# A two-layer diffusion backbone on one core: the first stage with TensorE's order written out, tokens loaded where the low parts go, seven strip buffers, and selector products for the strips' sums

## The chip, the cores and the metric

One core of a Trainium2 chip runs the whole program. The metric is the device time of one execution in microseconds, median of the runs; the profile shows one more execution of the same program. TensorE is called PE below, VectorE DVE, ScalarE ACT, GpSimd POOL, and SP is the engine that issues most of the loads.

## The reference

512 tokens (256 latent, 256 context) of width 2048 go through two layers. Layer 0 is bidirectional retention, layer 1 windowed attention. Each layer begins alike: an RMS norm of the tokens, times a gain and a scale, plus a shift, where scale, shift and a later gate are products of SiLU(c) with a large matrix `ada_w`, one set for the latent tokens and one for the context.

```python
c_act, cc_act = jax.nn.silu(c), jax.nn.silu(c_ctx)
...
mod_l = c_act @ ada_w[i] + ada_b[i]          # mod_c likewise from cc_act
sh_l, sc_l, gt_l = jnp.split(mod_l, 3, axis=-1)
h_l = _rms_norm(x, norm_gain[i]) * (1 + sc_l[:, None]) + sh_l[:, None]
h_c = _rms_norm(ctx, norm_gain[i]) * (1 + sc_c) + sh_c
...
p = h @ w_in                                  # queries, keys, values, gate of layer 0
```

## The kernel before, in words

Everything is held transposed: width on the partitions in 16 blocks of 128 (called kb), the 512 tokens along the free axis. A float32 product is made of three products of a rounded type: each operand is split into a high part and a low part (`split`, L109 to L111: ACT casts to the high part at L110, DVE subtracts at L107), and `mm3` (L126 to L132) issues high times high, high times low and low times high. Weights come in pieces of 128 x 1024 (512 KB) through `load_w` (L120): three raw buffers, three high and three low ones.

The **first stage**, which the change rewrites, is L273 to L390. It does four things.

- *Tokens.* Eight DMAs bring the tokens into `xT`. ACT squares each of 16 blocks (L323, L326), DVE adds the squares up (L327), and `token_rstd` (L220) turns the sum into one factor per token: four products with a column of ones (L228), a power on POOL (L217), four transposes (L233). ACT copies the result to `rB` (L329). Between the adds DVE works through a chain of small operations for the decays of the retention (L290 to L317), which POOL's powers interrupt.
- *Strips.* `strip_part(u, g)` brings a quarter of the ada_w columns of two blocks (1 MB, `araw`, four buffers, L344) and multiplies it with the padded SiLU(c) (L346): four products side by side, each into 32 rows of one PSUM tile. After the fourth quarter ACT copies the tile (L351), PE transposes it in four pieces (L355), DVE sums the four groups of rows (L358), adds the bias and makes shift and gain (`ada_mod`, L248).
- *Modulation.* For each block and each kind of token (L236 to L245): DVE scales (L241), ACT adds the shift and rounds to the high part (L243), DVE makes the low part (L244).
- *Products.* The queries' and keys' columns of head 0 and of the next chunk: two weight pieces per pair of blocks. The first piece accumulates in four PSUM tiles through all 16 blocks (`qk0`); the second starts anew for each pair of blocks, and DVE adds each finished tile to `qk1` in SBUF (L386). Five PSUM tiles have the tag acc; `qk0` holds four of them through the stage, so that the second piece's tiles go through the one that is left, and the last of four through a tile of the tag pm (three in all, shared with the strips and transposes).

The loop runs over 64 groups (8 pairs of blocks x 2 pieces x 4 column slices), and a table (`DUE`) says before which group a quarter of the next strip is issued. The framework's scheduler then decides how the instructions of each engine stand; each engine carries its own out in order. SP's loads stand in one queue too: a load that has no free buffer holds all behind it. After the stage, the values' chunk starts (`gemm_ts`, L180), and the rest of the program follows.

Of the kernel before, what the change touches and what calls it, by code (L numbers as in the profile page):

```python
# [20 lines left out]
KB = 16  # L21
# [5 lines left out]
DUE = (0, 2, 4, 5)  # L27
DUE0 = (0, 2, 4, 5)
# [20 lines left out]
V_END = V_KG + 128  # L49
# [3 lines left out]
def backbone(ctx: ExitStack, tc, xT_d, w0_d, wo0_d, w1_d, wo1_d, adaS_d, adaB_d,  # L53
# [46 lines left out]
    hT = r1.tile([P, 2, KB, T], F32R, name="hT")  # L100
    hT_h, hT_l = hT[:, 0], hT[:, 1]


    h1 = hT.rearrange("p a k t -> p (a k t)").rearrange("p (k s a t) -> p k s a t", k=KB, s=2, a=2)
# [22 lines left out]
    def mm3(ps, a, b, start, stop, skip=False):  # L127

        (ah, al), (bh, bl) = a, b
        nc.tensor.matmul(ps, lhsT=ah, rhs=bh, start=start, stop=False, skip_group_check=skip)  # L130
        nc.tensor.matmul(ps, lhsT=ah, rhs=bl, start=False, stop=False, skip_group_check=skip)  # L131
        nc.tensor.matmul(ps, lhsT=al, rhs=bh, start=False, stop=stop, skip_group_check=skip)  # L132
# [26 lines left out]
    def gemm_ws2(w_d, chunk, nkp, s, hook=None, pre=None):  # L159
# [3 lines left out]
        for kp in range(nkp):  # L163
# [3 lines left out]
            for j in range(4):  # L167
                js = slice(j * P, (j + 1) * P)
                for k2 in range(2):
                    kb = 2 * kp + k2  # L170
                    nc.tensor.matmul(accs[j], lhsT=wh[:, k2, js], rhs=h1[:, kb, s].rearrange("p a t -> p (a t)"),  # L171
                                     start=(kb == 0), stop=False)
                    nc.tensor.matmul(accs[j][:, 0:L], lhsT=wl[:, k2, js], rhs=h1[:, kb, s, 0],  # L173
# [21 lines left out]
    def h_mov(kb):  # L195
        return hT_h[:, kb, :], hT_l[:, kb, :]

    def h_stat(kb, t):
        s = slice(t * P, (t + 1) * P)
        return hT_h[:, kb, s], hT_l[:, kb, s]  # L200

    def h1_stat(kb, t):
        s = slice(t % 2 * P, (t % 2 + 1) * P)
        return h1[:, kb, t // 2, 0, s], h1[:, kb, t // 2, 1, s]
# [15 lines left out]
    def token_rstd(pool, parts, blocks=(0, 4)):  # L220
# [10 lines left out]
        bp = m_tile()  # L231
        for t in range(n):
# [3 lines left out]
    def modulate(t, src, kb, gs, sh, rB, kinds=(0, 1), layer=0):  # L236

        for s in kinds:
            c = slice(s * L, (s + 1) * L)
            hi, lo = (h1[:, kb, s, 0], h1[:, kb, s, 1]) if layer else (hT_h[:, kb, c], hT_l[:, kb, c])  # L240
            nc.vector.scalar_tensor_tensor(out=t[:, c], in0=src[:, c], scalar=gs[:, kb, s:s + 1],  # L241
                                           in1=rB[:, c], op0=ALU.mult, op1=ALU.mult)
            nc.scalar.activation(hi, t[:, c], AF.Identity, bias=sh[:, kb, s:s + 1])  # L243
            nc.vector.scalar_tensor_tensor(out=lo, in0=t[:, c], scalar=sh[:, kb, s:s + 1],  # L244
                                           in1=hi.bitcast(F32), op0=ALU.add, op1=ALU.subtract)  # L245

# [26 lines left out]

    with tc.tile_pool(name="pa", bufs=1) as pa:
        xT = pa.tile([P, KB, T], F32, name="xT")
        for i in range(8):
            nc.sync.dma_start(out=xT[:, 2 * i:2 * i + 2, :], in_=xT_d[:, 2 * i:2 * i + 2, :])
        nc.sync.dma_start(out=cst, in_=cst_d)


        nc.scalar.activation(cact.rearrange("p k t -> p (k t)"), vec[:, V_C:V_C + 32], AF.Silu)
        cpad = wide("aacc1", "cpad").rearrange("p (k t) -> p k t", t=32)
        nc.gpsimd.memset(cpad, 0.0)
        nc.vector.tensor_copy(cpad[:, :, 0:2], cact)

# [33 lines left out]

        ssq = wide("rows", "ssq")  # L320
        for i in range(KB):
            if i == 0:
                nc.scalar.activation(ssq, xT[:, 0, :], AF.Square)  # L323
                continue
            sq = wide("pt", "sq", 2)
            nc.scalar.activation(sq, xT[:, i, :], AF.Square)  # L326
            nc.vector.tensor_tensor(out=ssq, in0=ssq, in1=sq, op=ALU.add)  # L327
        rB = wide("aacc0", "rB")
        nc.scalar.copy(rB, token_rstd(pb, [ssq]))  # L329


        units = [[2 * k, 2 * k + 1] for k in range(8)]
        strips = {}

        def strip_part(u, g):
# [4 lines left out]
            if g == 0:  # L340
                strips[u] = m_tile()
            ap_ = strips[u]
            raw = pa.tile([P, 4, 512], F32, name="araw", tag="araw", bufs=4)
# [4 lines left out]
            if g < 3:  # L348
                return
# [644 lines left out]
```

## Time and profile before

| | us |
|---|---|
| median of 3 runs (2017.89 to 2020.73) | 2019.93 |
| the profiled execution, by the same clock | 2020.57 |
| its span, first to last instruction | 2018.6 |
| first product of the stage with tokens, L130 | starts at 34.48 |
| first product of the values' chunk | starts at 161.76 |

Rows of the time line have the start in us, the duration, the engine, the line, the operation, what it writes and reads, a count, and in brackets how long the engine had sat idle before and what ended that. A row with a count above one merges neighbours, and its duration is the time that they cover. Products are pipelined, so that the distance from one start to the next, not the duration, is what one costs. Rows of the table by stretches have, behind the stretch, the busy time and the count for PE, its weight loads, DVE, ACT and POOL, and then the clock granted to PE, the share of the DMA engines, and GB/s.

### The profile page before, as it was taken

To read this page: it belongs to the slowest core of one execution; us is meant where nothing else is said; L and a number is where in the kernel's file an instruction comes from. 1 tells how busy PE (TensorE), PEld (TensorE's weight loads), DVE (VectorE), ACT (ScalarE), POOL (GpSimd) and SP (SyncE) were. 2 spreads that over 40 slices of the span, in tenths; PEclk is the share of its full clock that TensorE was granted. 3 is DMA by queue.
4 is the path that set the end of the run, shared out by engine and by line. 5 is a ranking of instruction groups with operands and counts; after the bars stand their busy time and mean duration, and the time that the engine had idled before them with its cause. 6 is when DMAs were issued, how large, how long until landed. Compare 5 with 4: busy or idle time off the path is not lost.

```text
span 2018.6 us, 24747 instructions
## 1 busy us (share of the span) xinstructions
PE 1986.9 (98%) x9312; PEld 1620.5 (80%) x9312; DVE 1160.1 (57%) x2324; ACT 708.4 (35%) x1080; POOL 239.7 (12%) x89
## 2 busy tenths in 40 slices
PE   5999999999999999999999999999999999999999
PEld 2558888888888888888888888888888888888887
DVE  4556323778678688686465244432232665777754
ACT  3224223233232232232332233422221434766653
POOL 6500402203104004004000000000000010000001
PEclk9999999999999999999999999999999999999999
DMA  9873224565556656555555334733333334444455
GB/s 362 334 267 111 86 92 150 180 197 168 183 176 189 183 170 188 183 179 181 188 183 163 113 104 147 265 121 99 110 105 95 104 98 147 139 141 130 151 190 168
DMA packets 112711, 330.10 MB, mean 164 GB/s; under 512 B 12112, under 2 KB 18384, under 8 KB 107856
## 3 DMA queue, kind: packets, MB, share of 16 engines
q1 hardware_dynamic: 103376, 315.94, 48.0%
q10 hardware_dynamic: 9216, 12.59, 1.7%
q8 instruction: 73, 1.20, 0.2%
q14 instruction: 46, 0.38, 0.1%
HBM read 315.90 MB, written 12.58 MB: 163 GB/s over the span
## 4 chain that ended last, share of the span: by engine, by line
PE 96%; DVE 1%; DMA 1%; issue 0%; ACT 0%; POOL 0%; SPq 0%; DVEq 0%; POOLq 0%; ACTq 0%
PE acc L130 26%; PE acc L131 25%; PE acc L132 25%; PE acc L171 6%; PE acc L173 3%; PE pm L130 2%; PE pm L131 2%; PE pm L132 2%; PE pm L346 2%; DMA wraw<-uT_d 1%; PE pm L843 1%; PE pm L560 1%; DVE ssq L327 0%; DMA xT<-in_xT 0%; PE pm L773 0%
## 5 line engine op out<-in xcount | busy, mean ns | idle before, releaser
L107 DVE TENSOR_TENSOR wl<-wraw,wh 128x1024 fp32r<-128x1024 f32 x368 | 451.2, 1227 | 621.6 <-ACT wh L110 621.0
L110 ACT CAST wh<-wraw 128x1024 fp32r<-128x1024 f32 x368 | 386.9, 1052 | 948.4 <-PE acc L132 494.1
L130 PE MATMUL acc<-wh,hT 128*128 128x512 f32 x1280 | 501.5, 392 | 0.0
L132 PE MATMUL acc<-wh,hT 128*128 128x512 f32 x1280 | 498.7, 390 | 0.0
L131 PE MATMUL acc<-wl,hT 128*128 128x512 f32 x1280 | 498.6, 390 | 0.0
L439 DVE SCALAR_TENSOR_TENSOR ajunk<-abraw,crow 128x512 bf16<-128x512 f32 x448 | 308.8, 689 | 11.2 <-ACT crow L428 2.8
L130 PE MATMUL acc<-hT,wh 128*128 128x512 f32 x752 | 298.1, 397 | 2.6 <-ACT wh L110 1.9
L131 PE MATMUL acc<-hT,wh 128*128 128x512 f32 x752 | 294.8, 392 | 0.0
L132 PE MATMUL acc<-hT,wl 128*128 128x512 f32 x752 | 289.8, 390 | 0.0
L132 PEld LDWEIGHTS acc<-wh,hT 128*128 128x128 f32 x1280 | 240.2, 188 | 50.9 <-DVE hT L244 0.7
L130 PEld LDWEIGHTS acc<-wh,hT 128*128 128x128 f32 x1280 | 240.5, 188 | 48.4 <-issue 0.3
L131 PEld LDWEIGHTS acc<-wl,hT 128*128 128x128 f32 x1280 | 240.5, 188 | 48.4 <-DVE wl L107 0.2
L502 POOL TENSOR_TENSOR dd<-two,dd 128x128 f32<-128x128 f32 x8 | 167.5, 20944 | 601.6 <-DVE dd L500 601.6
L130 PEld LDWEIGHTS acc<-hT,wh 128*128 128x128 f32 x752 | 141.6, 188 | 53.7 <-DVE qk L386 7.2
L171 PE MATMUL acc<-hT,wh 128*128 128x512 f32 x512 | 182.7, 399 | 0.0
L131 PEld LDWEIGHTS acc<-hT,wh 128*128 128x128 f32 x752 | 141.7, 188 | 32.1 <-issue 4.2
L132 PEld LDWEIGHTS acc<-hT,wl 128*128 128x128 f32 x752 | 141.3, 188 | 30.3 <-issue 0.8
L217 POOL TENSOR_TENSOR rs<-ms,mhalf 128x1 f32<-128x1 f32 (+2 forms) x47 | 40.8, 868 | 1023.6 <-DVE ms L211 673.7
L173 PE MATMUL acc<-hT,wl 128*128 128x256 f32 x512 | 144.0, 281 | 0.0
L171 PEld LDWEIGHTS acc<-hT,wh 128*128 128x128 f32 x512 | 96.2, 188 | 22.7
L173 PEld LDWEIGHTS acc<-hT,wl 128*128 128x128 f32 x512 | 96.7, 189 | 0.7
L131 PE MATMUL acc<-r_l,wh 128*128 128x512 f32 (+1 forms) x188 | 70.7, 376 | 0.0
(208 smaller groups left out, 1836.4 us busy)
## 6 DMA issues: line engine op xcount, KB each, us to landing
wraw<-in_w SPq DMA_DIRECT2D x272, 512.0 KB, 3.5
abraw<-in_adaB SPq DMA_DIRECT2D x256, 256.0 KB, 3.3
wraw<-in_wo SPq DMA_DIRECT2D x96, 512.0 KB, 3.5
araw<-in_adaS SPq DMA_DIRECT2D x32, 1024.0 KB, 7.5
uT_d<-ue ACTq DMA_DIRECT2D x32, 256.0 KB, 2.1
wraw<-uT_d SPq DMA_DIRECT2D x16, 512.0 KB, 4.1
xT<-in_xT SPq DMA_DIRECT2D x8, 512.0 KB, 8.4
x<-in_xT SPq DMA_DIRECT2D x4, 1024.0 KB, 7.5
```

What stands on the lines that cost most here:

```text
L107: return nc.vector.tensor_tensor(out=out, in0=a, in1=hi.bitcast(F32), op=ALU.subtract)
L110: nc.scalar.copy(hi, src)
L130: nc.tensor.matmul(ps, lhsT=ah, rhs=bh, start=start, stop=False, skip_group_check=skip)
L131: nc.tensor.matmul(ps, lhsT=ah, rhs=bl, start=False, stop=False, skip_group_check=skip)
L132: nc.tensor.matmul(ps, lhsT=al, rhs=bh, start=False, stop=stop, skip_group_check=skip)
L171: nc.tensor.matmul(accs[j], lhsT=wh[:, k2, js], rhs=h1[:, kb, s].rearrange("p a t -> p (a t)"), start=(kb == 0), stop=False)
L173: nc.tensor.matmul(accs[j][:, 0:L], lhsT=wl[:, k2, js], rhs=h1[:, kb, s, 0], start=False, stop=(kb == 2 * nkp - 1))
L217: nc.gpsimd.tensor_tensor(out=rs, in0=ms, in1=mhalf.to_broadcast([P, n]), op=ALU.pow)
L346: nc.tensor.matmul(ap_[32 * j:32 * j + 32, :n], lhsT=cpad[:, 4 * g + j, :], rhs=raw[:, j, :n], start=(g == 0), stop=(g == 3))
L439: nc.vector.scalar_tensor_tensor(out=junk, in0=raw, scalar=1.0, in1=crow[:, t, q * 512:(q + 1) * 512], op0=ALU.mult, op1=ALU.mult, accum_o ...
L502: nc.gpsimd.tensor_tensor(out=dd, in0=two.to_broadcast([P, P]), in1=dd, op=ALU.pow)
L560: nc.tensor.transpose(tp[:, q * P:(q + 1) * P], sg[:, q, f * P:(f + 1) * P], ident)
```

## The change

- The tokens are not loaded into a tile of their own. The low parts of the modulated tokens become eight tiles of two blocks (`hl`), and seven of them first hold the raw tokens (`xp`); the first two blocks have a small tile (`x01`). The high parts are a tile of their own (`hT_h`), and the second layer's views of the same space (`h1`) are rewritten to match.
- The squares are taken two blocks at a time (128 x 1024), the last two blocks one at a time.
- With the room that this leaves there are seven `araw` buffers in the place of four. The first pair of blocks is cut in two units, each with half strips (256 columns, rows of 1 KB).
- The order is written out: `part0` makes the first piece's products of one block, by passes (high x high for all four slices, then high x low, then low x high), `part1` the second piece's, `strip` all quarters of a strip in one go. `issue_after` ties each batch of products to the last one before it, so that PE's order is that of the code.
- The sums over the four groups of rows are made by PE: the copied strip is the stationary operand, and a constant of two columns (`V_SEL`, ones in rows 0, 32, 64, 96 and 1, 33, ...) picks and adds. The result has two columns per product instead of 128, and DVE makes gain and shift straight from it; the reduction is gone.
- The chain of the decays moves from the start to the middle of the stage (`decay_powers`, at u = 4).

The core of the diff:

```diff
-    hT = r1.tile([P, 2, KB, T], F32R, name="hT")
+    hT_h = r1.tile([P, KB, T], F32R, name="hT_h")
+    hl = [None] * 8
...
+        x01 = pa.tile([P, 2, T], F32, name="x01")
+        xp = [x01] + [r1.tile([P, 2, T], F32, name="xp", tag=f"hl{k}") for k in range(1, 8)]
...
+        for i in range(9):
+            k0, nk = (2 * i, 2) if i < 7 else (i + 7, 1)
+            src = xp[k0 // 2][:, k0 % 2:k0 % 2 + nk, :]
+            nc.sync.dma_start(out=src, in_=xT_d[:, k0:k0 + nk, :])
...
-            raw = pa.tile([P, 4, 512], F32, name="araw", tag="araw", bufs=4)
+                raw = pa.tile([P, 4, 512], F32, name="araw", tag="araw", bufs=7)
...
-            for b in range(nb):
-                nc.tensor.transpose(tp[:, b * P:(b + 1) * P], ev[:, b * P:(b + 1) * P], ident)
...
+            with after():
+                for b in range(2 * nb):
+                    last = nc.tensor.matmul(tp[:, 2 * b:2 * b + 2], lhsT=ev[:, b * P:(b + 1) * P],
+                                            rhs=vec[:, V_SEL:V_SEL + 2], start=True, stop=True)
...
+        def part1(kbs, js_=range(4)):
+            for j in js_:
+                ps = m_tile() if j % 2 else acc_tile()
...
+        bp = token_rstd(pb, [ssq], between=first)
+        strip(0, [2, 3])
+        strip_copy(0)
+        strip_turn(0, bp)
+        rB = wide("aacc0", "rB")
+        nc.scalar.copy(rB, bp)
+        part0(0)
+        strip(1, [0, 1])
+        w[1] = load_w(w0_d[3, 0])
+        strip(1, [2, 3])
+        strip_copy(1)
+        part1([0], [0])
+        strip_turn(1, rB)
+        part1([0], [1, 2, 3])
+        part0(1)
+        strip(2, [0, 1])
...
+        for u in range(2, 9):
+            a_, b_ = units[u]
+            w[0], w[1] = w2, load_w(w0_d[3, u - 1])
+            part0(a_)
+            if u < 8:
+                strip(u + 1, [0, 1])
+                w2 = load_w(w0_d[0, u])
+                if u == 4:
+                    with tc.issue_after(last_lo[0]):
+                        decay_powers()
+                strip(u + 1, [2, 3])
+                strip_copy(u + 1)
+                part0(b_, [0])
+                strip_turn(u + 1, rB)
+                part0(b_, [1, 2])
+            else:
+                part0(b_)
+            part1([a_, b_])
```

The instructions of PE in one pair of blocks, before (a stretch with two quarters of a strip; x4 counts the four products of a quarter; the transposes follow a few rows later):

```order
L346 MATMUL pm<-araw,cpad 32x512 x4
L130 MATMUL acc<-hT,wh 128x512
L131 MATMUL acc<-hT,wh 128x512
L132 MATMUL acc<-hT,wl 128x512
L130 MATMUL acc<-hT,wh 128x512
L131 MATMUL acc<-hT,wh 128x512
L132 MATMUL acc<-hT,wl 128x512
L346 MATMUL pm<-araw,cpad 32x512 x4
L130 MATMUL acc<-hT,wh 128x512
L131 MATMUL acc<-hT,wh 128x512
L132 MATMUL acc<-hT,wl 128x512
L130 MATMUL acc<-hT,wh 128x512
```

The same place of the changed program: the four quarters stand together (x16), then one pass of the next block, the selector products (L393), two more passes, and the second piece's products:

```order
L423 MATMUL acc<-hT_h,wl 128x512 x4
L375 MATMUL pm<-araw,cpad 32x512 x16
L423 MATMUL acc<-hT_h,wh 128x512 x4
L393 MATMUL pm<-vec,ev 128x2 x4
L423 MATMUL acc<-hl,wh 128x512 x4
L423 MATMUL acc<-hT_h,wl 128x512 x4
L135 MATMUL acc<-hT_h,wh 128x512
L136 MATMUL acc<-hl,wh 128x512
L137 MATMUL acc<-hT_h,wl 128x512
L135 MATMUL acc<-hT_h,wh 128x512
```

The quarters are no longer spread among the products, and the selector products stand where the transposes stood. On DVE, before, with the numbers of the tiles (qk1 adds come from PSUM tiles acc and pm): the first add of a pair of blocks stands ahead of the strip's reduction, the second right behind it.

```order
L386 TENSOR_TENSOR qk1_228<-acc_692,qk1_228 128x512
L358 TENSOR_REDUCE tv_713<-pm_708 128x8
L251 TENSOR_TENSOR sh0_89<-tv_713,vec_72 128x4
L251 TENSOR_TENSOR gs0_90<-tv_713,vec_72 128x4
L386 TENSOR_TENSOR qk1_228<-acc_732,qk1_228 128x512
L254 SCALAR_TENSOR_TENSOR gs0_90<-gs0_90,vec_72 128x4
L241 SCALAR_TENSOR_TENSOR ht_718<-xT_107,gs0_90,rB_208 128x256 x2
```

DVE in the changed program, the same place (wl_505 is the low part of a weight piece, hl_453 the low part of the tokens; acc_470 is the first of the four second-piece tiles, acc_486 the third):

```order
L398 SCALAR_TENSOR_TENSOR gs0_90<-pm_439,ab1_122,vec_72 128x2 x2
L264 TENSOR_TENSOR sh0_89<-pm_439,vec_72 128x4
L257 SCALAR_TENSOR_TENSOR ht_447<-xp_109,gs0_90,rB_216 128x256 x2
L257 SCALAR_TENSOR_TENSOR ht_450<-xp_109,gs0_90,rB_216 128x256 x2
L112 TENSOR_TENSOR wl_505<-wraw_502,wh_504 128x1024
L250 SCALAR_TENSOR_TENSOR hl_453<-ht_447,sh0_89,hT_h_98 128x256 x2
L250 SCALAR_TENSOR_TENSOR hl_453<-ht_450,sh0_89,hT_h_98 128x256 x2
L440 TENSOR_TENSOR qk1_155<-acc_470,qk1_155 128x512
L440 TENSOR_TENSOR qk1_155<-pm_478,qk1_155 128x512
L440 TENSOR_TENSOR qk1_155<-acc_486,qk1_155 128x512
```

The adds now stand behind the scaling, a weight's low part and the tokens' low parts of the next strip. On ACT the order at this place is copy of the strip (L384), cast of a weight piece to its high part (L115), four activations (L249). Behind the stage each engine's instructions stand as before.

The third place is on DVE where the decays' chain has gone. Before, its end stands ahead of the first strip's reduction (L358), at the start of the stage:

```order
L306 TENSOR_TENSOR lacc<-t,lacc 128x16
L307 TENSOR_SCALAR lg_97<-lacc 128x16
L311 TENSOR_TENSOR gam_96<-cst,lg_97 128x32 x2
L498 TENSOR_SCALAR dd<-cst,lg_97 128x128 x2
L500 SCALAR_TENSOR_TENSOR dd<-cst,lg_97,dd 128x128 x2
L358 TENSOR_REDUCE tv<-pm 128x8
```

In the changed program 33 instructions of it, one of which needs POOL's power of `e`, stand as a block between a weight's low part and the gain of the strip that is turned at u = 4; its end:

```order
L307 TENSOR_TENSOR lacc_661<-t_659,lacc_661 128x16
L308 TENSOR_SCALAR lg2_97<-lacc_661 128x16
L312 TENSOR_TENSOR gam16_96<-cst_74,lg2_97 128x32 x2
L598 TENSOR_SCALAR dd_1456<-cst_74,lg2_97 128x128
L398 SCALAR_TENSOR_TENSOR gs0_90<-pm_715,ab1_122,vec_72 128x2 x2
L264 TENSOR_TENSOR sh0_89<-pm_715,vec_72 128x4
```

What stood among the squares at the start now stands ahead of the gain of one strip.

More of the change, by code (lines that the diff above doesn't have):

```diff
@@ L48 @@
 V_KG = V_QG + 128
-V_END = V_KG + 128
+V_SEL = V_KG + 128
+V_END = V_SEL + 2
 @with_exitstack
@@ L271, in wide, with decay_powers @@
         return pb.tile([P, 512], F32, name=name, tag=tag, bufs=bufs)
[L274 to L284, printed above, removed]
+    def decay_powers():
         xl = vec[:, V_LGT:V_LGT + 16]
```

181 lines of the change are left out of this document (115 added, 66 removed).

## The prediction

> **What bounds the kernel now.** I read the page first, then PE's time line through one pair of blocks of the first stage, then the starts and ends of the stage, then DVE and ACT in it.
>
> ```profile
> span 2018.6 us, 24747 instructions
> PE 96%; DVE 1%; DMA 1%; issue 0%; ACT 0%; POOL 0%; SPq 0%; DVEq 0%; POOLq 0%; ACTq 0%
> ```
>
> The chain of work that ended last runs on PE for 96% of the span. So a change pays where it shortens PE's own row of work or a gap in it. The stage at hand ends for PE when the values' products begin:
>
> ```profile
> 20.28 1.87 PE L228 MATMUL pm<-ones,ssq 128*128 128x1 f32 x8 [20.28 <-DVE ssq L327]
> 23.49 1.12 PE L233 MATMUL pm<-ident,rs 128*128 128x128 f32 x4 [1.35 <-POOL rs L217]
> 34.48 0.80 PE L130 MATMUL acc<-hT,wh 128*128 128x512 f32 x1 [1.93 <-ACT wh L110]
> 161.76 0.39 PE L130 MATMUL acc<-wh,hT 128*128 128x512 f32 x1
> ```
>
> PE does next to nothing for 34.48 us, then works 127.3 us to the stage's end at 161.76. Since the order of everything behind the stage is kept, the sum is about that end alone: what it moves, the kernel moves. Within the stage, DVE's reduction of a strip comes back every 16.46 us, and PE's rows between say what fills that:
>
> ```profile
> 97.20 0.19 DVE L358 TENSOR_REDUCE tv<-pm 128x8 f32<-128x32 f32 x1 [1.89 <-PE pm L355]
> 113.66 0.19 DVE L358 TENSOR_REDUCE tv<-pm 128x8 f32<-128x32 f32 x1 [1.89 <-PE pm L355]
> ```
> ```profile
> 94.19 0.40 PE L132 MATMUL acc<-hT,wl 128*128 128x512 f32 x1
> 94.52 1.06 PE L346 MATMUL pm<-araw,cpad 128*32 128x512 f32 x8
> 95.51 0.50 PE L130 MATMUL acc<-hT,wh 128*128 128x512 f32 x1
> 95.85 0.40 PE L131 MATMUL acc<-hT,wh 128*128 128x512 f32 x1
> ...
> 96.33 0.40 PE L130 MATMUL acc<-hT,wh 128*128 128x512 f32 x1
> 96.56 0.60 PE L355 MATMUL pm<-ident,ev 128*128 128x128 f32 x4
> 96.92 0.47 PE L131 MATMUL acc<-hT,wh 128*128 128x512 f32 x1
> 97.23 0.40 PE L132 MATMUL acc<-hT,wl 128*128 128x512 f32 x1
> ...
> 104.61 0.40 PE L132 MATMUL acc<-hT,wl 128*128 128x512 f32 x1
> ...
> 108.07 0.39 PE L132 MATMUL acc<-hT,wl 128*128 128x512 f32 x1
> ```
>
> From 104.61 to 108.07 lie 15 steps between dense products: 0.231 us each. Around one quarter of a strip, 94.19 to 95.85 takes 1.66 where two steps alone would take 0.46, so a quarter costs 1.20. Around four transposes, 96.33 to 97.23 takes 0.90 for two steps: 0.44. A pair of blocks is then 48 x 0.231 + 4 x 1.20 + 0.44 = 16.3 of the 16.46. PE is the bound, with almost no gap; loads are not.
>
> **The change, part by part.** *Strips in one go.* Once a strip's first products had got going in this trace, weight loads of its bursts (four side by side) came this far apart:
>
> ```profile
> 27.59 0.12 PEld L346 LDWEIGHTS pm<-araw,cpad 128*32 128x32 f32 x4 [0.31 <-issue]
> 28.02 0.12 PEld L346 LDWEIGHTS pm<-araw,cpad 128*32 128x32 f32 x4 [0.31 <-issue]
> ```
>
> A burst is 0.43 and a quarter two of them. Sixteen products in a row cost 1.20 + 3 x 0.86 = 3.78 against 4.80: 1.0 saved in each of seven full strips.
>
> *Selector products.* Their like, a float32 product with 128 x 128 stationary and one moving column, stands once between warm products (x4 rows are two products):
>
> ```profile
> 1584.07 0.58 PE L228 MATMUL pm<-ones,ssq 128*128 128x1 f32 x4
> 1584.51 0.36 PE L130 MATMUL acc<-r2y_h,wh 128*128 128x256 f32 x1
> ```
>
> The four rows take 0.44, so that the eight of four products take 0.88, and with edges like a quarter's (0.99 for two bursts of 0.43, so 0.13) 1.0. The transposes cost 0.44: 0.56 lost per strip. Strip and sum together gain 0.45 per pair of blocks.
>
> *The order.* PE now waits wherever its next row waits. I follow one strip from the moment X at which PE goes on behind the selector products, with these rows:
>
> ```profile
> 33.39 1.03 ACT L110 CAST wh<-wraw 128x1024 fp32r<-128x1024 f32 x1
> 114.92 1.28 DVE L241 SCALAR_TENSOR_TENSOR ht<-xT,gs,rB 128x256 f32<-128x256 f32 x3
> 116.12 1.27 DVE L244 SCALAR_TENSOR_TENSOR hT<-ht,sh,hT 128x256 fp32r<-128x256 f32 x3
> 118.77 0.68 DVE L386 TENSOR_TENSOR qk<-pm,qk 128x512 f32<-128x512 f32 x1
> 119.37 2.35 DVE L107 TENSOR_TENSOR wl<-wraw,wh 128x1024 fp32r<-128x1024 f32 x2
> ```
>
> PE: eight products of the passes until X+1.96, the first two tiles of the second piece (12 products) until X+4.73; then the third tile. It needs the acc tile that the first one used, so it waits for DVE's add of the first. DVE's rows ahead of that add: gain and shift to X+0.5, four scalings by 0.40 to X+2.2, then the weight's low part. That needs ACT's cast, which needs the high part's buffer free, that is the second pass read: X+1.2, cast to X+2.3. So the low part stands from X+2.3 to X+3.48 (half of 2.35), four low parts of tokens by 0.395 to X+5.06, the add 0.69 to X+5.74, and PE goes on at X+5.8: **1.07 lost per pair**, at u = 2 to 7. Before, the add stood ahead of the reduction or right behind it, and a waiting product let others pass in the scheduler's order. A pair so costs 11.07 + 3.78 + 1.0 + 1.07 = 16.92 against 16.46. The bounds of the wait are nothing (if the add is not behind) and 2.2 (if ACT's cast and its four activations run 1.1 later, by a late weight).
>
> *The decays.* In the old place they stand among the squares, where PE has nothing. In the new one they stand ahead of one strip's gain:
>
> ```profile
> 4.17 2.91 POOL L295 TENSOR_TENSOR e<-two,ax 128x16 f32<-128x16 f32 x1 [2.43 <-DVE cpad L284]
> 22.46 0.19 DVE L302 TENSOR_TENSOR lacc<-lacc,t 128x16 f32<-128x16 f32 x1
> 22.68 0.17 DVE L303 TENSOR_SCALAR lacc<-lacc 128x16 f32<-128x16 f32 x1
> ```
>
> Dependent small steps are 0.21 apart. The chain is three of them, POOL's 2.91, 26 more and three others: 0.7 + 3.0 + 5.5 + 0.5 = 9.7. DVE can begin 2.2 behind the end of the last pair's products (a weight's cast and low part come first), and so ends at 11.9; the strip's gain would have been due at 8.6 (12 products, the strip, a pass, the selector products, and 0.17 until their last result, as 1584.65 lies behind 1584.51). The delay of 3.3 goes into the wait above, less 0.15 of slack: **3.15 once**.
>
> *The start.* ACT waits for tokens no longer than this:
>
> ```profile
> 8.03 1.15 ACT L326 ACTIVATE sq<-xT 128x512 f32<-128x512 f32 x2 [1.60 <-DMA xT<-in_xT]
> ```
>
> From the second load's landing at 8.03 on, DVE is what the squares wait for. Six adds of 1024 columns behind each other take 1.18 + 0.1 each (as a weight's low part, which has their shape), behind a first square of 1.05 (as the cast above, of the same shape): 9.1 to 16.8. One fold and two single adds of 0.69 + 0.08 bring the sum to 19.1, 1.2 ahead of before (bounds: 17.0, if only one square and one add follow tokens that land at 15.7, that is 1.7 behind the 14 us by which the row below has their bytes moved; and 20.3). From the first statistics product to the power's end lie 3.2, as in the rows 20.28 and 23.49: 22.3. The four transposes now wait behind half of the first strip, at the slow step till 22.8, and end at 23.9. The other half, its copy and two selector products at the slow step take 1.4, 0.4 and 0.8: 26.5. Gain, two scalings and the second activation of one block take 0.35, 0.9 and 0.5: **28.25** in the place of 34.48, a gain of 6.2 (bounds 4 and 8.5). In front of the old start PE had been idle for 1.93, and then ran slowly:
>
> ```profile
> 34.00:36.00 2.00, 1.52 (x4) 1.23 (x5) 2.00 (x4) 0.93 (x2) 1.92 (x3) 0.51 1.01 426
> 36.00:38.00 2.00, 2.00 (x7) 1.61 (x6) 0.12 (x1) 0.00 (x0) 2.00 (x1) 0.64 0.99 410
> 22.00:24.00 2.00, 0.65 (x4) 0.57 (x5) 1.58 (x11) 0.00 (x0) 1.01 (x1) 1.00 1.06 434
> ```
>
> The granted clock, the third column from the end, is 0.51 and 0.64 there: 1.52 x 0.49 + 2 x 0.36 = 1.5 lost. I charge the same to the new start, which has a similar gap ahead of it. The seven buffers and the half strips act through landings alone; what they could cost stands with the rivals, and the pairs' loads have cover: PE's work per pair exceeds theirs (5.2 MB at the last row's 434 GB/s is 12 us).
>
> *The sum.* Start 28.25; 384 products at 3.46 / 15, 88.6; slow clock 1.5; the half strip of the second unit 2.1 (eight bursts of half the length and the same edges); seven strips 26.5; selector products 0.6 + 7.0; six waits 6.4 and 0.45 for the second block's activations, which stand behind two copies on ACT; decays 3.15. That is **164.5** against 161.76: 2.8 us later. The sum stands against the profiled execution's 2020.57, of which the span is 2018.6; the median of the runs is 0.64 below it. I take 2019.93 + 2.8 = 2022.7. By the same terms the old stage comes to 34.48 + 88.6 + 1.5 + 27 x 1.20 + 7 x 0.44 = 160.1, 1.7 short of the trace, so terms that small escape this sum.
>
> **The rivals.** *DVE is not in the way* (faster). If the adds reach DVE ahead of the low parts, or the decays run in its idle time, 6.4 + 3.15 fall away: the stage ends at 155.0, 6.8 earlier, 2013.1. For it speaks that DVE had idled 1.89 us ahead of each reduction (97.20, 113.66). Against it, DVE's rows are fixed, and the add stands last.
>
> ```profile
> 0.00:14.00 14.00, 0.00 (x0) 0.00 (x0) 6.60 (x24) 7.45 (x12) 4.08 (x8) 1.00 0.87 318
> ```
>
> *The loads are late* (slower). By the fourth unit's strip 19.9 MB must have come; with 4.45 MB moved by 14 us (318 GB/s, above), a landing in time for its last quarter (54.2, less the same allowance of 1.7) needs 400 GB/s. The old stage had 434 at 22 to 24, but the half strips come in rows of 1 KB, which no row here shows alone. At 360, the last quarter lands 4.4 late and the stage ends at 168.9: 2027.1. Below 400 GB/s it decides. *The clock falls at each wait* (slower). A gap of 1.93 us ended in a clock of 0.51. If gaps of 1.07 do so too, 1.5 comes on top at up to seven waits: up to 2033; if only the decays' 4.2 us do, 2024.2. [...] That the change does not do what it says is excluded by the order of the rows.
>
> **How the numbers follow.** A measurement of this kernel tells about 0.2% from no change, 4.0 us: 2015.9 to 2024.0 counts as the same. The forecast (2019 to 2026) has 0.50, of which 0.37 lies within the bound and 0.13 above. DVE not in the way has 0.23 (0.20 faster, 0.03 within); late loads 0.16 and the clock 0.08, both slower; 0.03 for something slower that I don't see. That makes faster 0.20, same 0.40, slower 0.40. The likeliest case's own range is 2019 to 2026; with the rivals' middles it becomes 2013.0 to 2028.5.
>
> **What would show it.** The first product with tokens at 28 (26 to 30). A gap of about 1 us on PE ahead of the third tile of the second piece in six pairs, released by DVE's add, and one of 4 at u = 4. A strip of 16 products at 3.6 to 3.8; four selector products at 1.0. The values' products from 164.5. Wrong it would be if PE's waits were for DMA, if the pairs came at 15.9 without a wait, or if anything behind the stage changed.

## The result and the profile after

The changed kernel takes 2024.71 us (median of 9 runs, 2024.2 to 2026.51), the kernel before in the same comparison 2018.58 (9 runs, 2015.73 to 2020.73). The ratio is 1.0033, with a 95% interval of 1.0022 to 1.0043: a third of a per cent slower, some 6 us, where 2.8 were forecast. The page of the changed kernel has the same bound as before, with less of it:

```profile
span 2022.7 us, 24898 instructions
PE 93%; DMA 2%; DVE 2%; issue 1%; ACT 1%; SPq 0%; POOL 0%; ACTq 0%; POOLq 0%; DVEq 0%
```

DVE's share of the chain of waits goes from 1% to 2%. Where it stands is seen in PE's time line (start, duration, engine and line, operation, tiles, and in brackets the idle time ahead with what ended it). First the start and the end of the stage, then one pair of blocks, then the waits ahead of the third tile of a second piece:

```profile
18.76 1.87 PE L234 MATMUL pm<-ones,ssq 128*128 128x1 f32 x8 [18.76 <-DVE ssq L352]
28.00 2.07 PE L423 MATMUL acc<-hT_h,wh 128*128 128x512 f32 x4 [1.77 <-ACT hT_h L249]
54.97 1.06 PE L375 MATMUL pm<-araw,cpad 128*32 128x512 f32 x8 [0.45 <-DMA araw<-in_adaS]
...
69.28 3.64 PE L375 MATMUL pm<-araw,cpad 128*32 128x512 f32 x32
79.09 0.39 PE L137 MATMUL pm<-hT_h,wl 128*128 128x512 f32 x1
80.48 0.50 PE L135 MATMUL acc<-hT_h,wh 128*128 128x512 f32 x1 [1.01 <-DVE qk L440]
80.82 0.40 PE L136 MATMUL acc<-hl,wh 128*128 128x512 f32 x1
86.14 3.64 PE L375 MATMUL pm<-araw,cpad 128*32 128x512 f32 x32
100.47 0.80 PE L135 MATMUL acc<-hT_h,wh 128*128 128x512 f32 x1 [4.13 <-DVE qk L440]
101.06 0.63 PE L136 MATMUL acc<-hl,wh 128*128 128x512 f32 x1
101.49 0.63 PE L137 MATMUL acc<-hT_h,wl 128*128 128x512 f32 x1
106.86 1.08 PE L423 MATMUL acc<-hl,wh 128*128 128x512 f32 x4
120.00 0.50 PE L135 MATMUL acc<-hT_h,wh 128*128 128x512 f32 x1 [1.01 <-DVE qk L440]
167.51 0.39 PE L135 MATMUL acc<-wh,hT_h 128*128 128x512 f32 x1
```

The first product with tokens comes at 28.00 in the place of 34.48. A pair takes 16.86 (69.28 to 86.14) in the place of 16.46, and in it PE idles for 1.01 until DVE's add of the first tile is done. At the fourth pair this wait is 4.13. There are six such waits, five of about 1.0 and this one. PE waits for a strip's load once, 0.45. The stage ends at 167.51 in the place of 161.76, 5.75 later. The spans of the two profiles differ by less, 4.1: the rest of the program, whose order is kept, took 1856.8 before and 1855.2 after, and between 1855.2 and 1857.3 in all the profiles of this document. So single profiles are compared within the stage, and whole times by the medians. DVE's time line tells why the fourth pair waits:

```profile
74.87 0.35 DVE L398 SCALAR_TENSOR_TENSOR gs<-pm,ab,vec 128x2 f32<-128x2 f32 x2 [6.07 <-PE pm L393]
...
89.18 0.17 DVE L297 TENSOR_SCALAR t<-e 128x16 f32<-128x16 f32 x1 [3.01 <-POOL e L296]
...
94.91 0.28 DVE L598 TENSOR_SCALAR dd<-cst,lg 128x128 f32<-128x128 f32 x1
95.11 0.34 DVE L398 SCALAR_TENSOR_TENSOR gs<-pm,ab,vec 128x2 f32<-128x2 f32 x2
```

In an ordinary pair DVE idles for 6.07 ahead of a strip's gain. The decays fill this and run over: 16.86 behind 74.87 the gain was due at 91.73, and it comes at 95.11, 3.4 late. What PE does behind this wait is the surprise. Its products follow each other by 0.43 (101.06, 101.49), not by 0.23, and the table of stretches has the granted clock, the third column from the end, at half:

```profile
98.00:100.00 2.00, 0.00 (x0) 0.00 (x0) 2.00 (x6) 0.00 (x0) 2.00 (x1) 0.83 0.38 74
100.00:102.00 2.00, 1.53 (x4) 1.24 (x5) 1.82 (x5) 0.00 (x0) 2.00 (x1) 0.50 1.06 430
...
106.00:108.00 2.00, 2.00 (x9) 1.59 (x9) 1.91 (x2) 0.66 (x1) 2.00 (x1) 0.97 0.00 0
```

From 100.47 to 106.86 PE does 16 products in 6.39 us. At 0.227 each they are 3.63, so that the half clock costs **2.8 us**. Whether the idle time is what brings it, the experiments tell.

### The profile page after: what moved, and what is told of

Its sections match the earlier page's. It is cut to its first block, busy times and chain, and to the rows that moved or that the text cites. A ratio compares the mean times of both kernels' runs of the same rounds, so it can differ in the third digit from the quotient of the medians.

```text
span 2022.7 us, 24898 instructions
## 1 busy us (share of the span) xinstructions
PE 1985.5 (98%) x9376; PEld 1630.2 (81%) x9376; DVE 1163.5 (58%) x2316; ACT 706.7 (35%) x1074; POOL 239.6 (12%) x89
## 4 chain that ended last, share of the span: by engine, by line
PE 93%; DMA 2%; DVE 2%; issue 1%; ACT 1%; SPq 0%; POOL 0%; ACTq 0%; POOLq 0%; DVEq 0%
PE acc L135 24%; PE acc L137 24%; PE acc L136 24%; PE acc L176 6%; PE acc L178 3%; PE pm L135 3%; PE pm L136 3%; PE pm L137 2%; PE acc L423 2%; PE pm L375 1%; DMA wraw<-uT_d 1%; PE pm L944 1%; PE pm L660 1%; DMA araw<-in_adaS 1%; DMA wraw<-in_w 0%
## 5 line engine op out<-in xcount | busy, mean ns | idle before, releaser
L115 ACT CAST wh<-wraw 128x1024 fp32r<-128x1024 f32 x368 | 387.1, 1052 | 1002.1 <-PE acc L137 494.9
L137 PE MATMUL acc<-wh,hl 128*128 128x512 f32 x1216 | 473.9, 390 | 0.0
L135 PE MATMUL acc<-wh,hT_h 128*128 128x512 f32 x1088 | 426.6, 392 | 0.0
L136 PE MATMUL acc<-wl,hT_h 128*128 128x512 f32 x1088 | 423.8, 390 | 0.0
L135 PE MATMUL acc<-hT_h,wh 128*128 128x512 f32 x672 | 264.6, 394 | 9.1 <-DVE qk L440 9.1
L137 PEld LDWEIGHTS acc<-wh,hl 128*128 128x128 f32 x1216 | 228.2, 188 | 48.7 <-DVE hl L250 0.8
L136 PE MATMUL acc<-hl,wh 128*128 128x512 f32 x672 | 262.2, 390 | 0.0
L137 PE MATMUL acc<-hT_h,wl 128*128 128x512 f32 x672 | 261.1, 390 | 0.0
L135 PEld LDWEIGHTS acc<-wh,hT_h 128*128 128x128 f32 x1088 | 204.4, 188 | 41.4 <-issue 0.3
L136 PEld LDWEIGHTS acc<-wl,hT_h 128*128 128x128 f32 x1088 | 204.4, 188 | 41.0
L602 POOL TENSOR_TENSOR dd<-two,dd 128x128 f32<-128x128 f32 x8 | 167.3, 20922 | 537.7 <-DVE dd L600 537.7
L136 PEld LDWEIGHTS acc<-hl,wh 128*128 128x128 f32 x672 | 126.5, 188 | 25.4
L176 PE MATMUL acc<-hl,wh 128*128 128x512 f32 x256 | 92.2, 401 | 0.0
L176 PE MATMUL acc<-hT_h,wh 128*128 128x512 f32 x256 | 89.3, 394 | 0.0
L135 PE MATMUL acc<-wh,hl 128*128 128x512 f32 x192 | 75.5, 393 | 0.0
```

Of the source, the lines that this page charges most:

```text
L115: nc.scalar.copy(hi, src)
L137: return nc.tensor.matmul(ps, lhsT=al, rhs=bh, start=False, stop=stop, skip_group_check=skip).ins
L176: nc.tensor.matmul(accs[j], lhsT=wh[:, k2, js], rhs=h1(kb, s).rearrange("p a t -> p (a t)"), start=(kb == 0), stop=False)
L602: nc.gpsimd.tensor_tensor(out=dd, in0=two.to_broadcast([P, P]), in1=dd, op=ALU.pow)
```

## Experiments

The theory after the result: the change loses 5 x 1.0 in waits for DVE's add, which exist because the third tile uses the bank of the first, 4.1 in the wait at the decays, and 2.8 by the half clock that the long idle time brings. The main rivals: the half clock has another cause; the waits, once removed, only move; the loads are what bounds the stage.

The runs stand beside different sets of runs of the kernel before, whose medians go from 2018.58 to 2020.54. So the ratios are what is compared; 0.001 is 2.0 us. The table's last three columns come from one profile each. The first product with tokens came between 27.27 and 30.15 in the changed kernels, so a stage's end is read together with it.

| kernel | median, us | ratio to before, 95% interval | first product with tokens, us | stage end, us | period of a pair, us |
|---|---|---|---|---|---|
| the change | 2024.71 | 1.0033 (1.0022 to 1.0043) | 28.00 | 167.51 | 16.86 |
| decays in two halves | 2020.16 | 1.0001 (0.9993 to 1.0010) | 27.87 | 161.36 | 16.89 |
| third tile's bank | 2018.30 | 0.9992 (0.9983 to 1.0001) | 28.74 | 159.85 | |
| both | 2012.10 | 0.9965 (0.9953 to 0.9978) | 30.15 | 156.35 | 15.58 |
| both, transposes | 2011.68 | 0.9964 (0.9950 to 0.9978) | 27.91 | 153.70 | 15.23 |
| the change, decays at start | 2020.81 | 1.0009 (1.0000 to 1.0017) | 30.15 | 163.60 | 16.88 |
| both, strips spread | 2016.12 | 0.9983 (0.9974 to 0.9992) | 28.66 | 157.87 | 16.30 |
| both, four buffers | 2018.55 | 0.9992 (0.9983 to 1.0001) | 29.44 | 160.69 | 15.59 |
| combination | 2009.87 | 0.9952 (0.9939 to 0.9964) | 27.42 | 151.07 | 15.15 |
| the change, wait filled | 2022.61 | 1.0013 (1.0004 to 1.0022) | 27.27 | 164.87 | |
| both, transposes, gain in one | 2010.17 | 0.9953 (0.9941 to 0.9966) | 29.38 | 152.11 | |
| combination, table later | 2010.43 | 0.9954 (0.9941 to 0.9966) | 28.39 | 151.17 | |
| the change, four buffers | 2032.38 | 1.0063 (1.0050 to 1.0075) | 28.75 | 174.03 | 16.87 |

### The decays in two halves

```diff
         for k in range(8, -1, -1):
+            if k == 6:
+                yield
...
-                if u == 4:
+                if u in (4, 5):
                     with tc.issue_after(last_lo[0]):
-                        decay_powers()
+                        next(powers, None)
```

> The decays' chain in two halves, the first (to the second of nine steps of the series) ahead of one strip's gain, the rest ahead of the next. Theory (the wait and the clock behind it): each half fits into DVE's idle time of 6.1 us ahead of a gain (74.87 in the trace of the change), so the wait of 4.13 at 100.47 becomes one of 1.0 like the others, and the granted clock stays at 1.0 there, where it was 0.50 for 12 products (0.427 in the place of 0.227 each, 2.8 lost). Both fall away: 3.1 + 2.8 = 5.9, 2018.8 us. Rival (the low clock comes from something else in that stretch): the wait shrinks, the low clock stays, 2021.6. Second rival (DVE does not set this wait): nothing moves, 2024.7.

Measured: 1.0001 in the place of 1.0033, 0.32% or 6.5 us, where 5.9 were expected. The wait is one like the others and the clock stays up:

```profile
96.90 0.50 PE L135 MATMUL acc<-hT_h,wh 128*128 128x512 f32 x1 [1.01 <-DVE qk L442]
```

So with the decays moved aside the change is level with the kernel before. The shared bank still costs its waits in it; what the change gains elsewhere makes up for them.

### Another bank for the third tile

```diff
-                ps = m_tile() if j % 2 else acc_tile()
+                ps = m_tile() if j in (1, 2) else acc_tile()
```

> The third of a second piece's four tiles takes a bank of the strips' set in the place of the one that the first tile used; the fourth takes that one. Theory (PE waits at the third tile for DVE's add because they share a bank): the add has six products more, 1.38 us, so the five waits of 1.0 are gone, and the decays' wait goes from 4.13 to 2.75. If an idle time of 2.75 still halves the clock: 2024.7 - 5.0 - 1.4 = 2018.3 us. If it needs more than that: 2.8 less, 2015.5. Rival (the wait only moves to the fourth tile or to the next strip): 2023 to 2025.

Measured: 0.9992, 0.41% less than the change. The five waits of 1.0 are gone, as the theory of the shared bank has it. The decays' wait is 3.55, not 2.75: in this kernel's order on DVE four tables of the decays (L598 and L600) stand ahead of the gain where one stood before.

```profile
99.12 0.50 PE L135 MATMUL acc<-hT_h,wh 128*128 128x512 f32 x1 [3.55 <-DVE qk L440]
```
```profile
92.78 0.54 DVE L598 TENSOR_SCALAR dd<-cst,lg 128x128 f32<-128x128 f32 x2
93.23 0.60 DVE L600 SCALAR_TENSOR_TENSOR dd<-cst,lg,dd 128x128 f32<-128x128 f32 x2
93.76 0.34 DVE L398 SCALAR_TENSOR_TENSOR gs<-pm,ab,vec 128x2 f32<-128x2 f32 x2
```
```profile
100.25:100.50 0.25, 0.25 (x3) 0.20 (x2) 0.01 (x1) 0.00 (x0) 0.25 (x1) 0.74 0.97 393
103.75:104.00 0.25, 0.25 (x2) 0.19 (x1) 0.00 (x0) 0.00 (x0) 0.25 (x2) 0.94 0.00 0
```

The clock still falls, but only from 100.37 on (0.74 in a quarter of a microsecond is 0.12 at full clock), 1.2 us after PE has begun again, and it is back at 103.78: 3.41 us, 1.7 of them lost. Whether 2.75 would have halved it isn't told by this run. That the median is the 2018.3 of the expectation is luck: the wait was 0.8 longer than expected and the half clock cost 1.1 less.

### Both

The two edits above together.

> Both of the edits. Theory: no wait of PE for DVE is left in the stage's pairs and no low clock behind one: 2024.7 - 5 x 1.0 - 4.1 - 2.8 = 2012.8 us, faster than the kernel before by some 5.8, as the rival of the prediction in which DVE is not in the way had it (2013.1). Rival (what the waits free is lost to loads that come too late for the faster pairs of 15.85 us): waits for the strips' loads appear, 2015 to 2019.

Measured: 0.9965, 7.1 us faster than the kernel before and 13.7 faster than the change, where 5.8 and 11.9 were expected. No wait for DVE's add is left, and a pair takes 15.58. That is 1.28 less than in the change, though the wait's row says 1.01. The rows of the change tell why: from the last product ahead of the wait to the first behind it is 1.39 (79.09, 80.48), and to the one after that 0.34 (80.82), where undisturbed products follow each other by 0.23. So a wait of 1.01 costs 1.27. The change is thus a gain with two small faults: this is the rival of the prediction in which DVE is not in the way (2013.1), reached by taking DVE out of it.

### Transposes again

```diff
-                    last = nc.tensor.matmul(tp[:, 2 * b:2 * b + 2], lhsT=ev[:, b * P:(b + 1) * P],
-                                            rhs=vec[:, V_SEL:V_SEL + 2], start=True, stop=True)
+                    last = nc.tensor.transpose(tp[:, b * P:(b + 1) * P], ev[:, b * P:(b + 1) * P], ident)
...
+            nc.vector.reduce_sum(...)
+            for kind in (1, 0):
+                ada_mod(kind, 0, kbs[0], nb, tv[:, :nb, kind, :], sh0, gs0, gt0)
```

> On top of both edits the four transposes, the reduction and the gain and shift of before in the place of the selector products. Theory (PE is then the bound, and a strip's sum costs 0.44 by transposes, 1.0 by selector products): seven strips by 0.55 and two halves by 0.28 go, DVE's chain gets 0.35 longer but has 6 us of idle time ahead of it: 2012.8 - 4.3 = 2008.5 us. Rival (the transposes' 0.44 held only between products that hide their weight loads; in a row of their own they cost as much as the selector products): 2012.8. Second rival (the longer chain brings the wait for the add back at the fourth tile): 2013 to 2015.

Measured: 0.9964, nothing gained against 0.9965. The pairs do get shorter, 15.23 against 15.58: selector products cost 0.35 per strip more than transposes (0.56 in the prediction). What seven pairs gain so, 2.5, is given back at the second full strip, where the order on DVE put a weight's low part and an add between gain and scaling, and PE waited:

```profile
47.36 1.22 DVE L112 TENSOR_TENSOR wl<-wraw,wh 128x1024 fp32r<-128x1024 f32 x1
48.56 0.69 DVE L440 TENSOR_TENSOR qk<-pm,qk 128x512 f32<-128x512 f32 x1
49.17 1.67 DVE L257 SCALAR_TENSOR_TENSOR ht<-xp,gs,rB 128x256 f32<-128x256 f32 x4
```
```profile
27.91 2.07 PE L423 MATMUL acc<-hT_h,wh 128*128 128x512 f32 x4 [2.11 <-ACT hT_h L249]
50.64 1.21 PE L423 MATMUL acc<-hT_h,wh 128*128 128x512 f32 x4 [1.71 <-ACT hT_h L249]
```

With 0.34 more at the start (2.11 for 1.77) that is 2.05 of the 2.5. The stage ends of the two profiles, 156.35 and 153.70, don't contradict this: from the first product with tokens on they are 126.20 and 125.79 us, and the rest of the difference lies ahead of it.

### The decays at the start

The series is called ahead of the squares, as in the kernel before; the part that needs the table of exponents stays at `u == 4`.

> The change with the decays' series again among the squares at the start, as in the kernel before; only its last part, which needs the table of exponents, stays at the fourth pair. Theory (the place of the decays cost 3.1 of wait and 2.8 of low clock, and bought a shorter start): the wait of 4.13 becomes 1.0 and the clock stays at 1.0, the first statistics product comes some 1.3 later (20.28 in the trace of before, 18.76 in that of the change): 2024.7 - 5.9 + 1.3 = 2020.1 us. Rival (the small steps fit between the squares' adds and cost nothing there): 2018.8. Second rival (every step counts there, 26 by 0.21): 2024.3.

Measured: 1.0009, against 1.0001 with the decays in two halves. The first statistics product comes at 20.92, later than in all twelve kernels with the decays in the pairs (17.86 to 19.75), so the small steps do delay the squares' sum.

```profile
20.92 1.87 PE L234 MATMUL pm<-ones,ssq 128*128 128x1 f32 x8 [20.92 <-DVE ssq L355]
```

In this profile that is 2.2 later than in the change. By the ratios the kernel stands 1.6 behind the one with the decays in two halves, but the two intervals overlap. What is clear is that the new place in one piece costs 4.8 more than the old place (1.0033 against 1.0009); that two halves beat the old place is likely and not shown.

### The strips spread again

```diff
-            part0(a_)
...
-                strip(u + 1, [0, 1])
+                part0(a_, [0])
+                strip(u + 1, [0])
+                part0(a_, [1])
+                strip(u + 1, [1])
+                part0(a_, [2])
```

> The kernel with both edits, with the strips of the pairs in three groups again (a quarter behind the first pass, a quarter behind the second, a half behind the third) in the place of one go. Theory (a change between strip and dense products costs 0.34): twelve more of these changes, 2012.1 + 4.1 = 2016.2 us. Rival (the 1.20 of a quarter in the kernel before came from other things, such as the scheduler's order around it): 2012.1.

Measured: 2016.12, 4.0 above the kernel with both edits, as expected (3.6 by the ratios). Its pairs come every 16.30 (99.08 to 115.38), 0.72 more for two more changes between strip and dense products: 0.36 each.

```profile
99.08 1.07 PE L377 MATMUL pm<-araw,cpad 128*32 128x512 f32 x8
...
115.38 1.06 PE L377 MATMUL pm<-araw,cpad 128*32 128x512 f32 x8
```

### Four buffers, with both edits and in the change

```diff
-                raw = pa.tile([P, 4, 512], F32, name="araw", tag="araw", bufs=7)
+                raw = pa.tile([P, 4, 512], F32, name="araw", tag="araw", bufs=4)
```

> The kernel with both edits, with four strip buffers in the place of seven. Theory (loads have cover: PE's work per pair of 15.6 exceeds the 12 of its loads): the loads of a strip are issued later by three quarters, and only at the start do a few waits for strips appear: 2012.1 to 2014. Rival (seven buffers carry the stage, since its loads ran at 410 to 420 GB/s from 28 to 80 us): waits for strips' loads on PE in every early pair, 2016 to 2020.

> The change with four strip buffers in the place of seven, and nothing else. Theory (with both edits four buffers gave four waits for loads, 4.9 in all, all before 62 us, where the change's own waits had hardly begun): the same waits, 2024.7 + 4.9 = 2029.6 us. Rival (the pairs' waits for DVE take in a part, as the loads catch up during them): 2026 to 2028. Second rival (loads have cover, as the prediction said): 2024.7.

Measured: 6.4 us more with both edits and 7.7 more in the change by the medians, 5.5 and 6.1 by the ratios. With four buffers the early strips' loads have no cover. With both edits, PE waits for strips:

```profile
46.16 1.06 PE L377 MATMUL pm<-araw,cpad 128*32 128x512 f32 x8 [1.86 <-DMA araw<-in_adaS]
48.66 1.06 PE L377 MATMUL pm<-araw,cpad 128*32 128x512 f32 x8 [1.44 <-DMA araw<-in_adaS]
61.65 1.06 PE L377 MATMUL pm<-araw,cpad 128*32 128x512 f32 x8 [1.39 <-DMA araw<-in_adaS]
```
```profile
28.00:40.00 12.00, 10.47 (x63) 7.38 (x64) 4.96 (x11) 5.41 (x11) 0.00 (x0) 0.86 0.81 280
```

The last column is the GB/s. Between 28 and 40 us the loads came to 280 GB/s, just when they should have run ahead. In the change, with seven buffers, SP waits in this stretch for PE to free a strip's buffer, 6.6 in two waits, but ten loads for strips had been issued by 25.1, and the loads come to 416. With both edits and seven buffers they come to 415:

```profile
28.00:40.00 12.00, 10.23 (x60) 7.45 (x61) 4.37 (x11) 3.95 (x8) 0.00 (x0) 1.00 1.04 415
```

Behind 62 us no wait for a load is left with four buffers either. In the change with four buffers the first two waits come too, and the clock falls:

```profile
45.52 1.07 PE L375 MATMUL pm<-araw,cpad 128*32 128x512 f32 x8 [1.90 <-DMA araw<-in_adaS]
48.04 1.93 PE L375 MATMUL pm<-araw,cpad 128*32 128x512 f32 x8 [1.45 <-DMA araw<-in_adaS]
```
```profile
46.00:50.00 4.00, 2.55 (x17) 0.30 (x9) 0.00 (x0) 0.00 (x0) 0.00 (x0) 0.57 1.01 418
50.00:54.00 4.00, 4.00 (x14) 3.52 (x15) 1.60 (x6) 1.60 (x3) 0.00 (x0) 0.50 1.00 414
```

The clock is at half for 10.2 us (46.55 to 56.79, of which PE worked 8.8). So 3.35 of waits and half of 8.8, 4.4, are added. But behind the wait at the decays less is lost here: the next wait's end comes 18.48 behind it (126.27) in the place of 19.53:

```profile
107.79 0.64 PE L135 MATMUL acc<-hT_h,wh 128*128 128x512 f32 x1 [4.14 <-DVE qk L440]
```

That gives back 1.05, and the change's wait of 0.45 for a load is gone: 6.25 in sum. From the first product with tokens to the stage's end the two profiles differ by 5.8 (145.28 and 139.51). The expectation, 4.9, had four waits and no clock in it. With both edits it was the rival's 2016 to 2020 that came, by its four waits alone (the three rows above and one of 0.21), 4.9 in sum: there the clock stayed up through almost the same two waits, 1.86 and 1.44:

```profile
46.00:50.00 4.00, 2.40 (x18) 0.61 (x19) 0.00 (x0) 0.15 (x1) 0.00 (x0) 1.00 1.01 420
```

### The combination

On top of both edits: transposes and reduction, but the gain in one operation for each block, and at the start half a strip ahead of the first products with tokens. The second expectation is for the same kernel without the early half strip, the third for the combination with one load moved.

```diff
-        part0(0)
         strip(1, [0, 1])
+        part0(0)
```

> Transposes and reduction as before, but the gain in one operation for each block as in the change, and the first half of the second strip ahead of the first products with tokens. Theory 1 (with four operations for gain and shift a weight's low part and an add got between gain and scaling at the second strip, 47.36 and 48.56 in that trace, and PE waited 1.71 at 50.64): this wait goes, -1.7. Theory 2 (PE is idle for 2.1 ahead of the first products with tokens, and half a strip fits in): -1.0, and another 1.7 where the clock then does not fall. Together 2011.7 - 2.7 = 2009.0 us, 2007.3 if the clock stays. Rival (the half strip's load is not there in time, and its products delay the first ones): 2010 to 2012.

> The combination without the early half strip: both edits, transposes and reduction, the gain in one operation for each block. Theory (a low part and an add between gain and scaling made the wait of 1.71 at the second strip of the kernel with transposes): 2011.7 - 1.7 = 2010.0 us. Rival (loads are the bound there by now, so that the wait comes back as one for a strip's load): 2011.5.

> The combination with the load of the table of constants (295 KB) moved from the second strip to the fourth pair, where it is first needed. Theory (the early strips wait for loads that run at 414 to 420 GB/s without a pause, two waits of 1.4): 295 KB less ahead of them are 0.7 us, 2009.9 - 0.7 = 2009.2 us. Rival (the waits have another cause than the amount of data ahead): 2009.9.

Measured: 0.9952, 0.9953 and 0.9954, the same within their intervals and the fastest here, 0.5% below the kernel before. The gain in one operation alone takes away the wait of 1.71, as theory 1 has it (2010.17, for 2010.0 expected). The early half strip does what theory 2 says, too: the idle time ahead of the first token products is 0.98, and they run at full clock (1.20 for four, 2.07 in the change). For that case 2007.3 was expected, and it did not come (2009.87): the gain is lost to the loads, which now bound the early strips:

```profile
27.42 1.20 PE L426 MATMUL acc<-hT_h,wh 128*128 128x512 f32 x4 [0.98 <-ACT hT_h L249]
42.09 1.06 PE L377 MATMUL pm<-araw,cpad 128*32 128x512 f32 x8 [1.44 <-DMA araw<-in_adaS]
54.57 1.07 PE L377 MATMUL pm<-araw,cpad 128*32 128x512 f32 x8 [1.37 <-DMA araw<-in_adaS]
```

Without the early half strip there is no wait for a load. With the table's load moved, the first of the two is 0.71, 0.7 shorter as expected for 295 KB, and the second 1.35; the median, 2010.43 for 2009.2 expected, doesn't show it.

### The wait filled with work

```diff
             for j in js_:
+                if kbs[0] == 6 and j == 2:
+                    junk = m_tile()
+                    with after():
+                        for _ in range(14):
+                            last = nc.tensor.matmul(junk, lhsT=wh[:, 0, 0:P], rhs=hT_h[:, kbs[0], :],
+                                                    start=True, stop=True)
+                    pe[0] = last.ins
```

> The change with fourteen products more, whose result nobody reads, ahead of the third tile of the second piece at the fourth pair, the place of the wait of 4.13. They give PE 14 x 0.227 = 3.2 us of work while it would wait for DVE anyway; the wait's end is set by DVE and stays. Theory (the idle time, not the wait, halves the clock, and that costs 2.8): the granted clock stays at 1.0 there, what is left of the wait is about 1.0, and the kernel gets faster by doing more: 2024.7 - 2.8 = 2021.9 us. Rival (the low clock has another cause, or costs nothing): 2024.7. Second rival (the added products delay what follows): 2026 to 2028.

Measured: 1.0013 against 1.0033. The kernel does 14 products more, and is faster. The wait's end is where it was (100.43, for 100.47), its idle part is 0.97, and the clock stays at 1.00:

```profile
96.13 3.33 PE L434 MATMUL pm<-hT_h,wh 128*128 128x512 f32 x14
100.43 0.50 PE L135 MATMUL acc<-hT_h,wh 128*128 128x512 f32 x1 [0.97 <-DVE qk L447]
```
```profile
100.00:102.00 2.00, 1.57 (x7) 1.31 (x8) 1.78 (x5) 0.00 (x0) 2.00 (x1) 1.00 1.04 418
```

From the end of the wait to the next strip's first product PE takes 5.67 here (100.43 to 106.10) and 8.32 in the change (100.47 to 108.79): 2.65 less for the same work. The ratios differ by 4.0 us, with intervals of 1.8 to 2.1 us each way. So it is PE's idleness that halves the clock here, and this costs about 2.7: the rival of another cause has fallen.

## Why the prediction was right and where it was wrong

- **The start**: 28.25 forecast, 28.00 measured, and the slow clock behind it as charged: half clock to about 31.1, some 1.5. That the two agree within 0.25 is luck in part: in seven other profiles with the same order ahead of this product it came between 27.27 and 30.15.
- **Pair and waits**: 16.92 forecast with a wait of 1.07; 16.86 with 1.01. That the cause is the bank shared by first and third tile, the second experiment showed. That the period is met so closely is luck. The sum has 16.92 - 1.07 = 15.85 for a pair without the wait, and it took 15.58 (the third experiment); and it took the wait for its idle time alone, while it costs 1.28. Of the 0.27 that the pair's work was too dear, 0.17 are the 48 dense products (0.227 apart, eleven steps from 76.59 to 79.09 in the change's trace, not 0.231). Selector products cost 0.35 more than transposes and not 0.56, and a change between strip and dense products 0.36 (the fourth and sixth experiments; 0.34 forecast).
- **The decays**: 3.15 forecast on top of a pair's wait; 4.13 - 1.01 = 3.12.
- **The step that failed** is the sum's clock term. It charged the slow clock once, at the start, and left the half clock behind the decays' wait to a rival with a chance of 0.08 and a price of 1.5 (2024.2). The half clock came, and costs 2.8. The price had been taken from a start where the clock was low for 3.4 us; here it was low for 6.8, of which PE worked 5.65. With 2.8 in it, the stage would have been forecast to end at 167.3 (164.5 + 2.8); it ended at 167.51. The wait of 4.2 was known when the sum was made, and what had come behind a shorter gap, 1.93, too (a clock of 0.51), so 0.08 was too small a chance.
- **That the pairs' loads have cover** was right in the result (one wait of 0.45), but the reason was not enough. Comparing bytes with PE's work per pair holds for the later pairs, which have no wait for a load even with four buffers, and leaves out that loads must first get ahead. With four buffers they don't, and the kernel is 6.1 slower by the ratios. The seven buffers are what holds the rival of late loads off.
- **DVE not in the way**: the two experiments on the waits reached 2012.1, for 2013.1 forecast for this rival.

The total was forecast at +2.8 and is +6.1 by the medians: 2.8 of the difference is the clock, and the remaining 0.5 is less than these medians can tell. The time itself, 2024.71, lies only 2.0 above the forecast 2022.7, because the kernel before came out 1.35 lower beside it than the 2019.93 that the sum started from. So the likeliest case's range, 2019 to 2026, held the time by its width and that shift, not because the sum was complete.

## What to carry to other kernels

Where TensorE's order is fixed, look at each wait in it (here five of about 1.0 and one of 4.13) for what stands ahead of the releasing operation on the other engine, and give the tile another bank or split the long chain. A wait of several microseconds on TensorE cost more than its length here: 2.8 of half clock came behind 4.13 and 1.7 behind 3.55. Add that to the sum, or fill the wait. A short wait, too, cost more than its idle row says (1.28 for 1.01). Buffers for loads should be counted by how far the loads must run ahead at the start, not by the mean rate alone: four in the place of seven cost the change 6.1 by the ratios.

## What the runs showed of the hardware

At the decays' wait in the change the clock falls at 99.30 and rises at 106.12, 6.82 apart:

```profile
99.25:99.50 0.25, 0.00 (x0) 0.00 (x0) 0.25 (x2) 0.00 (x0) 0.25 (x1) 0.61 1.49 213
106.00:106.25 0.25, 0.25 (x2) 0.17 (x2) 0.25 (x1) 0.25 (x1) 0.25 (x1) 0.74 0.00 0
```

With the third tile's bank changed it was low for 3.41 (100.37 to 103.78), and it fell 1.2 us after work had begun again. The decays' waits in these two kernels were of 4.13 and 3.55. In the change with four buffers the clock was low for 10.2 at the early strips, and in the kernel before for 3.4 at the start (34.04 to 37.46), so shorter gaps (1.90 and 1.93) were followed by half clock too. Ahead of the first token products a gap of 1.77 was, at once or within 0.8 us, in each of the eight traces in which the clock had been up before it (2.07 for four products in the change), and so were gaps of 1.98 and 2.11. A gap of 0.98 was not (1.20 for four). Nor did a gap's length alone decide it here: 1.77 was followed by half clock, and 1.90 in the change with four buffers, while 1.86 with both edits and four buffers and 1.71 with transposes were not. In each of the eight traces another 0.49 or 0.50 of idle time stands shortly ahead of the 1.77; whether that counts wasn't tried by itself, and why the clock was low for 3.4 us at one place and for 6.8 or 10.2 at another stays open.

The column of the granted clock missed one slow stretch. In the kernel with both edits it says 1.00 from 28 to 32 and on to 36, while the four products from 32.02 on take 1.91, against 1.09 for four at 41.81:

```profile
32.02 1.91 PE L425 MATMUL acc<-hl,wh 128*128 128x512 f32 x4
```
```profile
28.00:32.00 4.00, 2.23 (x6) 1.78 (x7) 2.46 (x7) 2.32 (x4) 0.00 (x0) 1.00 1.07 413
```

The first statistics product, ahead of which the twelve kernels with the decays in the pairs do the same work, came between 17.86 and 19.75 in their profiles. So a part of the scatter between runs, up to 1.9 us, arises before PE has begun.
